# Source order for VectorE and ScalarE in the gated-input stage of a streaming encoder layer, with small changes at its start and its end

## The chip, the cores and the metric

One core of a Trainium2 chip runs the whole layer in one launch. The metric is the device time of an execution in microseconds (us). Before the change it is 1996.45 us, the median of 3 runs (1996.19 to 1996.85).

## What is computed

A conformer layer for 256 prompt frames and 8 x 16 sample frames, 384 rows in all, in float32:

```python
h   = rmsnorm(x)
proj = h @ w_in          # GLU in | q | k | v | forget logits | gate A | gate B
u = glu_in[..., :D_CONV] * sigmoid(glu_in[..., D_CONV:])
a_out = silu(layernorm(causal_dwconv(ext(u), 31 taps))) @ conv_pw_out
b_out = attn_fn(rmsnorm(q), rmsnorm(k), v, log_sigmoid(f_logit)) @ w_att_out
x = x + (sigmoid(gate_a) * a_out + sigmoid(gate_b) * b_out) @ w_out
x = x + (silu(causal_dwconv(g_half, 3 taps)) * u_half) @ w_down     # of rmsnorm(x) @ w_up
```

There are 8 heads of 128. A prompt frame looks at the prompt up to itself, a sample frame at 128 cached frames of its stream and at its own 16. D_MODEL is 2048, D_CONV 1024, D_FF 5632.

## The kernel before

Every product with weights is made of three TensorE passes: the float32 weights are split by ScalarE into a rounded part `hi` (L148, a cast) and by VectorE into the rest `lo` (L149), activations likewise, and hi x hi, hi x lo and lo x hi are added in PSUM (L245 to L247 where the activations are stationary, L250 to L252 in the other form). Weights come as tiles `raw` of two k blocks, fetched in the order of a plan (L139, SyncE's queue) and split two to three tiles ahead of their use by `ahead`; 3 tiles of `raw`, 3 of `hi` and 3 of `lo` are held.

`gemm` walks over jobs; after each k block it calls `tick`, which advances side work by one step. In the **gated-input stage** (L778 and after) four jobs of 16 k blocks make 64 ticks of 12 matmuls of 384 columns; each job fills four accumulators `acc` and ends, at ticks 15, 31, 47 and 63, with an evacuation by `glu_evac`: two VectorE products into `sgb`, two sigmoids of ScalarE, and two VectorE products into `ut`. Beside it run two generators. `conv` issues the 31 taps of the causal convolution on VectorE (L754), from tick 24 on. `attention` runs the 8 heads, one every 6 ticks: for head h at tick 6h+6 `head_operands` (VectorE transposes the cached keys `kc` into `kTs`, L611, and copies the queries into `qz`), at 6h+9 `head_scores` (TensorE scores L622 to L630 into three PSUM tiles, VectorE adds the bias `bs` and takes the maximum, ScalarE the exponentials `pr`), at 6h+14 `head_probs` (TensorE transposes L649 and L652; ScalarE copies one result into `pT`, L650, and VectorE the other into `pz`, L653), at 6h+17 `head_out` and at 6h+19 `head_last`. The PSUM tiles of these steps, `misc`, come from a ring of three, and so the second score tile (L624) needs `pT` of the head before copied out, and the third one (L626, L630) its `pz`. The cached keys and values and the bias rows of the heads are loaded by SyncE's queue (`load_k`, four DMAs into one of two `kc`; `load_v`; `load_b`); the loads of the next head's keys are issued with `head_operands`.

The order within an engine is that of a scheduler, which goes by priorities: a step written under `high_priority(offset=n)` counts as if it stood n instructions earlier. Weight splits and fetches have 150 (SPLIT_AHEAD), attention steps 250 (ATT_AHEAD), evacuations of accumulators 400 (EVAC_AHEAD). TensorE alone is held to the order of the source. `queued` ties an instruction behind the one of its engine that was given to it before, and so orders the instructions given to it.

At the **start** everything is written in order (L302 to L330): x comes in chunks of 128 columns, its 256 prompt rows by one DMA and its 128 sample rows by another, all on SyncE's queue, among the first weight rows. `x_chunk` transposes one chunk on TensorE and scales it into `hT` (ScalarE L297, VectorE L298). At the **end** the down projection is added into `y` in tiles of 128 x 512, and each tile of the last sum goes out by a DMA of SyncE's queue (L1052, L1055).

Of the kernel before, what the change touches and what calls it, by code (L numbers as in the profile page):

```python
# [19 lines left out]
H = 8  # L20
# [13 lines left out]
SPLIT_AHEAD, ATT_AHEAD, EVAC_AHEAD = 150, 250, 400  # L34
# [6 lines left out]
def hybrid_step(  # L41
# [36 lines left out]

    mm = nc.tensor.matmul
    tr = nc.tensor.transpose  # L80
    tt = nc.vector.tensor_tensor
    stt = nc.vector.scalar_tensor_tensor
    ts = nc.vector.tensor_scalar
# [15 lines left out]
    def load_x(c, n):  # L99
# [12 lines left out]
    def newton_rsqrt(r, s, m):  # L112
        queued(nc.scalar.activation(s, m, AF.Sqrt), in_first())
        nc.vector.reciprocal(r, s)
# [31 lines left out]
    def split_rows(hi, lo, raw, o, k):  # L146
        first = in_first()
        queued(nc.scalar.copy(hi[:, k, :o], raw[:, k, :o]), first)  # L148
        queued(tt(lo[:, k, :o], raw[:, k, :o], f(hi[:, k, :o]), op=ALU.subtract), first)  # L149
# [77 lines left out]
    def gemm(jobs, sides=(), wide=False):  # L227
        for js in jobs:
# [4 lines left out]
            for j, k in [(j, k + i) for k in range(0, js[0]["nk"], 2) for j in js for i in range(2)]:  # L233
# [29 lines left out]
    def blocks(rows, put):  # L263
        src = rows.rearrange("p t (m b j) -> p b m t j", m=4, b=4)
        for b in range(4):
            for a in range(4):
                nc.vector.transpose(put(a, slice(32 * b, 32 * b + 32)), src[32 * a:32 * a + 32, b])  # L267
# [22 lines left out]
    def x_chunk(c):  # L290
# [5 lines left out]
        with tc.high_priority(offset=EVAC_AHEAD):  # L296
            queued(nc.scalar.activation(hi, ps[:, :NT], AF.Identity, scale=g))  # L297
# [4 lines left out]
    with tc.manual_schedule(engines={ENG.SP, ENG.Activation, ENG.DVE}):  # L302
        nc.vector.memset(junk[:, 0:1], 0.0)
# [18 lines left out]
        nc.vector.tensor_copy(gm[:], pv[:, :16])  # L322
# [3 lines left out]
        warm_up(FILL)  # L326
        split_rows(hi, lo, first, V_COLS[0][0][1], slice(1, 2))
        x_chunk(1)
# [11 lines left out]
    def over_partitions(dg, dst):  # L340
# [3 lines left out]
        nc.scalar.copy(dst, ps[:, :NT])  # L344
# [46 lines left out]
    def small_columns():  # L391
        ps = misc_tile()
        tr(ps[:, :R_N], vrow[:R_N, :], ident[:R_N, :R_N])
        nc.vector.tensor_copy(col[:], ps[:, :R_N])
        ts(qgs[:], col[:, R_QG:R_QG + 1], float(P) ** -0.5, None, op0=ALU.mult)

    def first_norm():
        for c in range(2, 16, 2):
# [6 lines left out]
            if c % 4 == 2:  # L405
                for t in range(NTT):
                    n = c // 4
                    sq = nc.scalar.activation(junk[:], xs[n][:, t, :], AF.Square, accum_out=ssx[:, t, n:n + 1])
# [9 lines left out]
        with tc.high_priority(offset=EVAC_AHEAD):  # L418
            nc.vector.tensor_reduce(mt[:], ssx[:], axis=mybir.AxisListType.X, op=ALU.add)
            ts(mt[:], mt[:], 1.0 / DM, EPS, op0=ALU.mult, op1=ALU.add)  # L420
            r = rsqrt(mt[:], [P, NTT], p_x0, "r1")
            nc.vector.tensor_copy(rs1[:], r[:])
# [14 lines left out]
    def tok_job(dst, c0, n, sq):  # L437
        d = job("B", 16, ha, tok_evac(dst, c0, n))

        def post():  # L440
            for t in range(NTT):
                for h in range(c0 // P, (c0 + n) // P):
                    jk = p_qkv.tile([P, P], F32, tag="jk", bufs=2, name="jk")
                    nc.scalar.activation(jk[:], dst[:, t, h * P:(h + 1) * P], AF.Square,
# [4 lines left out]
    def tok_evac(dst, c0, n, shared=True):  # L449
        def ev(t, ps):  # L450
            if shared and t % 2:
                ts(dst[:, t, c0:c0 + n], ps[:, :n], rs1[:, t:t + 1], None, op0=ALU.mult)
            else:
                queued(nc.scalar.activation(dst[:, t, c0:c0 + n], ps[:, :n], AF.Identity, scale=rs1[:, t:t + 1]),
# [16 lines left out]
    nc.scalar.activation(e[:], e[:], AF.Exp, scale=-1.0)  # L471
    ts(r[:], e[:], 2.0, None, op0=ALU.add)
    nc.vector.reciprocal(r[:], r[:])
# [27 lines left out]
    def bias_rows():  # L501
        for _ in range(6):
            yield
        for i in range(2):
# [3 lines left out]
            nc.vector.tensor_copy(cw[:, i * 124:(i + 1) * 124], ps[:, :124])  # L508
            nc.vector.tensor_copy(fw[:, i * 66:(i + 1) * 66], ps[:, 128:128 + 66])
# [5 lines left out]
        nc.scalar.activation(crow[:, :2 * P], ps[:H, :2 * P], AF.Copy, scale=-1.0)  # L515
        ps = misc_tile()
        mm(ps[:H, :P], lg[:, 2, :], bm[:], start=True, stop=True)
        nc.scalar.activation(crow[:, 2 * P:], ps[:H, :P], AF.Copy, scale=-1.0)
# [3 lines left out]
        nc.scalar.copy(drow[:], ps[:64, :P])  # L522
# [18 lines left out]
    def q_panel(n):  # L541
        blocks(qt[:, :, 512 * n:512 * (n + 1)], by_feature(attT[:, 4 * n:4 * n + 4]))
        for h in range(4 * n, 4 * n + 4):
            nc.scalar.activation(attT[:, h], attT[:, h], AF.Identity, scale=qgs[:])
# [64 lines left out]
    def head_past_keys(d):  # L609
        kTs = p_att.tile([P, 8, P], F32, tag="kTs", bufs=1, name="kTs")  # L610
        nc.vector.transpose(kTs[:].rearrange("p b k -> p (b k)"), kcs[d["h"]][:])  # L611
        d["kTs"] = kTs

    def head_operands(d):
        head_past_keys(d)
        d["bs"] = bss[d["h"]]
        nc.vector.tensor_copy(qz[d["h"] % 2][:, :, :, 0:16], by_stream(attT[:, d["h"], 2 * P:]))
# [489 lines left out]
```

## Time and profile before

| what | us |
|---|---|
| median of 3 runs | 1996.45 |
| the profiled execution's own time | 1998.56 |
| its span from first to last instruction | 1996.7 |
| TensorE busy | 1986.5 |
| VectorE busy | 1305.3 |
| ScalarE busy | 743.2 |
| idle time of TensorE put down to a wait, longest single one | 2.5 |

The profile is one execution. Its times start at the first instruction, and its own time lies 1.9 us above its span and 2.1 us above the median of the runs. In its rows PE is TensorE's matmuls, PEld its weight loads, DVE is VectorE, ACT ScalarE, POOL GpSimd, SPq the issue of DMAs by SyncE. A row of the timeline has the start, the duration, engine, line and operation, what it writes and reads, how many in a row, and in brackets the idle time just ahead of it and what ended it. A row of the windows has the busy share of each engine in a stretch, then the granted TensorE clock as a share of the full one, the mean share of the 16 DMA engines, and their GB/s.

### The profile page before, as it was taken

Reading aid. Unit: us, or ns where it says so; the run is one execution under the profiler, and the core shown is the slowest. Engines: PE = TensorE matmul, PEld = TensorE weight load, DVE = VectorE, ACT = ScalarE, POOL = GpSimd, SP = SyncE. Lnnn points to the kernel's source line nnn. Section 1 sums busy time; section 2 is a strip of 40 time slices with the busy share of each in tenths; the row PEclk is TensorE's granted clock in tenths of the full one; section 3 lists DMA queues with packets and bytes.
Section 4 is the critical chain, followed back from the end, with each engine's and each line's share of the span. In section 5 each row is a group of like instructions: output and inputs, shape, how many; then the busy total and the mean of one; then the engine's idle time right before and its main releaser. Section 6 shows DMA issues by size and latency. Waiting matters only on the chain.

```text
span 1996.7 us, 24449 instructions
## 1 busy us (share of the span) xinstructions
PE 1986.5 (99%) x9383; PEld 1676.0 (84%) x9383; DVE 1305.3 (65%) x1908; ACT 743.2 (37%) x1077; POOL 89.5 (4%) x216
## 2 busy tenths in 40 slices
PE   9999999999999999999999999999999999999999
PEld 9888999888888888888888888888888888888887
DVE  4455889788755487676867683377673376638663
ACT  5535354433334433344333432233332233323321
POOL 1000011100000000000000000010000000000000
PEclk9999999999999999999999999999999999999999
DMA  6564767444443334534344443444433444343443
GB/s 184 149 188 117 216 154 161 141 140 131 130 129 124 128 125 163 165 122 137 119 137 126 129 134 129 129 126 127 136 129 132 132 118 137 128 133 120 138 158 106
DMA packets 209254, 275.98 MB, mean 138 GB/s; under 512 B 55878, under 2 KB 96729, under 8 KB 209129
## 3 DMA queue, kind: packets, MB, share of 16 engines
q1 hardware_dynamic: 208817, 273.85, 46.0%
q8 instruction: 73, 1.20, 0.3%
q0 software_dynamic: 288, 0.57, 0.1%
q14 instruction: 44, 0.36, 0.1%
q10 hardware_dynamic: 32, 0.01, 0.0%
HBM read 266.98 MB, written 7.86 MB: 138 GB/s over the span
## 4 chain that ended last, share of the span: by engine, by line
PE 96%; DVE 2%; DMA 1%; issue 0%; SPq 0%; ACT 0%; DVEq 0%; ACTq 0%
PE acc L252 20%; PE acc L250 20%; PE acc L251 20%; PE misc L252 10%; PE misc L251 10%; PE misc L250 10%; PE acc L245 2%; PE acc L247 2%; PE acc L246 2%; DVE lo L149 1%; DMA raw<-in_w_in_dram 0%; DVE mixT L267 0%; DVE ut L754 0%; DMA vc<-in_cache_v_dram 0%; DMA bs<-c_dr 0%
## 5 line engine op out<-in xcount | busy, mean ns | idle before, releaser
L149 DVE TENSOR_TENSOR lo<-raw,hi 128x1024 fp32r<-128x1024 f32 (+2 forms) x481 | 580.5, 1207 | 530.7 <-ACT hi L148 526.8
L148 ACT CAST hi<-raw 128x1024 fp32r<-128x1024 f32 (+2 forms) x481 | 496.3, 1032 | 970.1 <-PE misc L252 841.1
L250 PE MATMUL acc<-hi,xg 128*128 128x512 f32 x704 | 274.9, 390 | 0.0
L252 PE MATMUL acc<-hi,xg 128*128 128x512 f32 x704 | 273.9, 389 | 0.0
L251 PE MATMUL acc<-lo,xg 128*128 128x512 f32 x704 | 273.9, 389 | 0.0
L250 PE MATMUL acc<-hi,hT 128*128 128x512 f32 (+1 forms) x512 | 193.0, 377 | 0.5 <-ACT hT L297 0.5
L252 PE MATMUL acc<-hi,hT 128*128 128x512 f32 (+1 forms) x512 | 190.4, 372 | 0.2
L251 PE MATMUL acc<-lo,hT 128*128 128x512 f32 (+1 forms) x512 | 190.3, 372 | 0.0
L250 PEld LDWEIGHTS acc<-hi,xg 128*128 128x128 f32 x704 | 132.1, 188 | 28.4
L754 DVE SCALAR_TENSOR_TENSOR ut<-ext,cw,ut 128x384 f32<-128x384 f32 x240 | 151.9, 633 | 6.0
L252 PEld LDWEIGHTS acc<-hi,xg 128*128 128x128 f32 x704 | 132.1, 188 | 27.5
L251 PEld LDWEIGHTS acc<-lo,xg 128*128 128x128 f32 x704 | 132.2, 188 | 27.1
L252 PE MATMUL misc<-hi,xg 128*128 128x512 f32 x352 | 137.0, 389 | 0.0
L250 PE MATMUL misc<-hi,xg 128*128 128x512 f32 x352 | 137.0, 389 | 0.0
L251 PE MATMUL misc<-lo,xg 128*128 128x512 f32 x352 | 136.9, 389 | 0.0
L250 PE MATMUL acc<-hi,act 128*128 128x512 f32 x352 | 136.9, 389 | 0.0
L251 PE MATMUL acc<-lo,act 128*128 128x512 f32 x352 | 136.9, 389 | 0.0
L252 PE MATMUL acc<-hi,act 128*128 128x512 f32 x352 | 136.9, 389 | 0.0
L267 DVE STREAM_TRANSPOSE extf<-tok 32x384 f32<-32x384 f32 x176 | 100.3, 570 | 30.9 <-ACT tok L988 28.2
L267 DVE STREAM_TRANSPOSE uT<-tok 32x384 f32<-32x384 f32 x176 | 100.3, 570 | 29.7 <-ACT tok L988 26.9
L250 PEld LDWEIGHTS acc<-hi,hT 128*128 128x128 f32 x512 | 96.2, 188 | 16.1 <-ACT hT L297 1.0
L252 PEld LDWEIGHTS acc<-hi,hT 128*128 128x128 f32 x512 | 96.1, 188 | 15.7 <-DVE hT L298 0.7
(325 smaller groups left out, 3133.8 us busy)
## 6 DMA issues: line engine op xcount, KB each, us to landing
raw<-in_w_up_dram SPq DMA_DIRECT2D x176, 512.0 KB
raw<-in_w_in_dram SPq DMA_DIRECT2D x96, 512.0 KB
raw<-in_w_down_dram SPq DMA_DIRECT2D x88, 512.0 KB
raw<-in_w_in_dram SPq DMA_DIRECT2D x64, 256.0 KB
raw<-in_w_out_dram SPq DMA_DIRECT2D x32, 512.0 KB
raw<-in_w_att_out_dram SPq DMA_DIRECT2D x16, 512.0 KB
raw<-in_conv_pw_out_dram SPq DMA_DIRECT2D x16, 512.0 KB
raw<-in_w_in_dram SPq DMA_DIRECT2D x23, 344.0 KB
```

Source lines behind the costliest of these rows:

```text
L148: queued(nc.scalar.copy(hi[:, k, :o], raw[:, k, :o]), first)
L149: queued(tt(lo[:, k, :o], raw[:, k, :o], f(hi[:, k, :o]), op=ALU.subtract), first)
L245: mm(o, hi[:, kk, s], ah, start=st, stop=False)
L246: mm(o, hi[:, kk, s], al, start=False, stop=False)
L247: mm(o, lo[:, kk, s], ah, start=False, stop=sp)
L250: mm(o, ah[:, s], hi[:, kk, :n], start=st, stop=False)
L251: mm(o, ah[:, s], lo[:, kk, :n], start=False, stop=False)
L252: mm(o, al[:, s], hi[:, kk, :n], start=False, stop=sp)
L267: nc.vector.transpose(put(a, slice(32 * b, 32 * b + 32)), src[32 * a:32 * a + 32, b])
L754: stt(o, v, wc, o, op0=ALU.mult, op1=ALU.add)
```

## The change

1. All VectorE and ScalarE calls go through a wrapper, `InOrder`. While the list `chained` holds something, each instruction is tied behind the one before it on its engine. The list is filled just ahead of the gated-input jobs and emptied after the last attention step; the evacuations of accumulators in `gemm` are exempt and keep their priority.
2. The attention steps lose their priority of 250. The scaling of the probabilities becomes a step of its own, one tick after the scores, with one reciprocal of 3 columns for three of 1. `load_k` comes two heads ahead in place of one, `load_b` with the scaling step; these loads, `load_v` and `load_state` get the priority of weight fetches.
3. At the start ScalarE's queue loads the sample rows of the first two x chunks, ScalarE's first activation follows behind them, and the second `x_chunk` comes ahead of the split of the second weight row.
4. At the end the very last tile is added and stored in two halves of 256 columns, the second by ScalarE's queue.

```diff
+    chained = []
+    class InOrder:
+        def __getattr__(self, name):
+            op = getattr(self.eng, name)
+            def call(*a, **kw):
+                d = op(*a, **kw)
+                if chained:
+                    queued(d)
+                return d
+            return call
+    dve, act = InOrder(nc.vector), InOrder(nc.scalar)
...
+    def load_x(c, n, sample=nc.sync):
...
-        queued(nc.sync.dma_start(xs[c // 4][:, 2, o:o + n * P], xin[2][:, cs]))
+        queued(sample.dma_start(xs[c // 4][:, 2, o:o + n * P], xin[2][:, cs]))
...
                 if sp:
+                    held, chained[:] = chained[:], []
                     with tc.high_priority(offset=EVAC_AHEAD):
-                        for m in range(nb):
+                        for m in range(len(ps)):
                             j["evac"](m, ps[m])
+                    chained[:] = held
...
-        nc.scalar.activation(junk[:, 1:2], junk[:, 0:1], AF.Identity)
-        load_x(0, 1)
         first = stream_tile()
         fetch_row(first, plan[0], 0)
-        load_x(1, 1)
+        load_x(1, 1, nc.scalar)
+        act.activation(junk[:, 1:2], junk[:, 0:1], AF.Identity)
...
+        x_chunk(1)
         split_rows(hi, lo, first, V_COLS[0][0][1], slice(1, 2))
-        x_chunk(1)
...
-            nc.vector.reciprocal(mx[:, i:i + 1], mx[:, 6 + i:7 + i])
-            nc.scalar.activation(v, v, AF.Identity, scale=mx[:, i:i + 1])
+    def head_scale(d):
+        pr, mx = d["pr"], d["mx"]
+        dve.reciprocal(mx[:, 0:3], mx[:, 6:9])
+        for i, (_, o, n) in enumerate(d["segs"]):
+            v = pr[:, o * P:(o + n) * P]
+            act.activation(v, v, AF.Identity, scale=mx[:, i:i + 1])
...
-                with tc.high_priority(offset=ATT_AHEAD):
-                    step(d)
-                if step is head_operands and d["h"] + 1 < H:
-                    load_k(d["h"] + 1)
-                if step is head_probs and d["h"] + 2 < H:
-                    load_b(d["h"] + 2)
+                step(d)
+                with tc.high_priority(offset=SPLIT_AHEAD):
+                    if step is head_operands and d["h"] + 2 < H:
+                        load_k(d["h"] + 2)
+                    if step is head_scale and d["h"] + 2 < H:
+                        load_b(d["h"] + 2)
...
+    load_k(1)
...
+    chained.append(True)
     gemm([job("A", 16, ha, glu_evac(g)) for g in range(4)], [att_steps, conv_steps])
     drain(att_steps)
+    chained.clear()
...
-                tt(ys, ps[:], ys, op=ALU.add)
+                parts = [(0, 512)] if not last or n < 3 or t < 2 else [(0, 256), (256, 256)]
+                for o, w in parts:
+                    tt(ys[:, o:o + w], ps[:, o:o + w], ys[:, o:o + w], op=ALU.add)
```

TensorE's instructions stand in the same order in both kernels. Three places on the other engines, in the order in which each engine issues them, follow. In the changed kernel all wrapped calls have the wrapper's line, L89; the numbers in tile names count up in the order of the source.

The first place is VectorE ahead of the last head's scores. `kTs_3409` and `kTs_3395` are the last head's keys, `lo_3513` and `lo_3493` the split of the weights that the tick of these scores fetches, `misc_3457` and `misc_3443` the transposed probabilities of the head before. Before:

```order
L149 TENSOR_TENSOR lo_3435<-raw_3431,hi_3434 128x1024
L754 SCALAR_TENSOR_TENSOR ut_1998<-ext_3079,cw_753,ut_1998 128x384
L653 COPY pz0_1992<-misc_3457 128x8x16
L754 SCALAR_TENSOR_TENSOR ut_1998<-ext_3079,cw_753,ut_1998 128x384
L149 TENSOR_TENSOR lo_3513<-raw_3509,hi_3512 128x1024
L611 STREAM_TRANSPOSE kTs_3409<-kc_3211 128x1024
```

After:

```order
L89 STREAM_TRANSPOSE kTs_3395<-kc_3020 128x1024
L89 COPY qz1_1991<-attT_150 128x8x16
L89 SCALAR_TENSOR_TENSOR ut_1998<-ext_2556,cw_753,ut_1998 128x384
L89 SCALAR_TENSOR_TENSOR ut_1998<-ext_3074,cw_753,ut_1998 128x384
L89 COPY attT_150<-misc_3412 128x128
L89 SCALAR_TENSOR_TENSOR ut_1998<-ext_2556,cw_753,ut_1998 128x384
L89 SCALAR_TENSOR_TENSOR ut_1998<-ext_3074,cw_753,ut_1998 128x384
L89 TENSOR_TENSOR lo_3421<-raw_3417,hi_3420 128x1024
L89 COPY pz0_1992<-misc_3443 128x8x16
```

The key transpose has moved from behind the weight split of the scores' own tick to its own tick, three ticks ahead of the scores.

The second place is ScalarE at the first evacuation, tick 15, where head 0's `pT` and head 1's scores lie too. `hi_2300` and `hi_2310` are the split of the weights fetched at tick 14. Before:

```order
L148 CAST hi_2261<-raw_2258 128x1024
L148 CAST hi_2300<-raw_2297 128x1024
L650 COPY pT_2316<-misc_2317 128x512
L707 ACT_TABLE_LOAD
L707 ACTIVATE sgb_2345<-sgb_2345 128x384
L707 ACTIVATE sgb_2348<-sgb_2348 128x384
```

After:

```order
L89 CAST hi_2271<-raw_2268 128x1024
L89 ACT_TABLE_LOAD
L89 ACTIVATE sgb_2348<-sgb_2348 128x384
L89 ACTIVATE sgb_2351<-sgb_2351 128x384
L89 CAST hi_2310<-raw_2307 128x1024
L89 COPY pT_2326<-misc_2327 128x512
L89 ACT_TABLE_LOAD
```

The evacuation's sigmoids have moved ahead of the cast of tick 14 and of `pT`. VectorE has the same shift there: its products into `sgb_2348`, `sgb_2351` and `ut_1998` now follow on `kTs_2287`, the keys of head 1, and stand ahead of `lo_2311` (the rest of `hi_2310`) and `pz0_1992`.

The third place is SyncE's queue around the fetch of the weights of tick 14 (`raw_2297` before, `raw_2307` after) and the keys of heads 2 and 3. Before:

```order
L139 DMA raw_2258<-in_w_in_dram 128x2x256 x2
L724 DMA sc_2000<-in_state_conv_dram 30x8x32 x3
L139 DMA raw_2297<-in_w_in_dram 128x2x256 x2
L724 DMA sc_2000<-in_state_conv_dram 30x8x32
L139 DMA raw_2390<-in_w_in_dram 128x2x256 x2
L597 DMA bs_2326<-c_dr_755 128x128
L598 DMA bs_2326<-c_dr_755 128x256
L599 DMA bs_2326<-c_dr_755 128x128
L600 DMA bs_2326<-d_dr_756 128x1x128
L587 DMA kc_2460<-in_cache_k_dram 32x32x32
```

After:

```order
L156 DMA raw_2268<-in_w_in_dram 128x2x256 x2
L606 DMA kc_2149<-in_cache_k_dram 32x32x32 x4
L616 DMA bs_2249<-c_dr_755 128x128
L617 DMA bs_2249<-c_dr_755 128x256
L618 DMA bs_2249<-c_dr_755 128x128
L619 DMA bs_2249<-d_dr_756 128x1x128
L606 DMA kc_2290<-in_cache_k_dram 32x32x32 x4
L156 DMA raw_2307<-in_w_in_dram 128x2x256 x2
L156 DMA raw_2387<-in_w_in_dram 128x2x256 x2
```

The fetch of tick 14 has moved behind the four key loads of head 3, `kc_2290`, whose buffer comes free when `kTs_2287` has read it.

More of the change, by code (lines that the diff above doesn't have):

```diff
@@ L147, in split_rows @@
         first = in_first()
-        queued(nc.scalar.copy(hi[:, k, :o], raw[:, k, :o]), first)
+        queued(act.copy(hi[:, k, :o], raw[:, k, :o]), first)
         queued(tt(lo[:, k, :o], raw[:, k, :o], f(hi[:, k, :o]), op=ALU.subtract), first)
@@ L610, in head_past_keys @@
         kTs = p_att.tile([P, 8, P], F32, tag="kTs", bufs=1, name="kTs")
-        nc.vector.transpose(kTs[:].rearrange("p b k -> p (b k)"), kcs[d["h"]][:])
+        dve.transpose(kTs[:].rearrange("p b k -> p (b k)"), kcs[d["h"]][:])
         d["kTs"] = kTs
@@ L793, in hybrid_step @@
         hi, lo = aHL[h // 4][:, 0, h % 4, :], aHL[h // 4][:, 1, h % 4, :]
-        nc.scalar.copy(hi, attT[:, h, :])
+        act.copy(hi, attT[:, h, :])
         tt(lo, attT[:, h, :], f(hi), op=ALU.subtract)
```

135 lines of the change are left out of this document (69 added, 66 removed).

## The prediction

> **What bounds the kernel now.** I read the page first: the engines' busy time, then the chain that ended last.
>
> ```profile
> PE 1986.5 (99%) x9383; PEld 1676.0 (84%) x9383; DVE 1305.3 (65%) x1908; ACT 743.2 (37%) x1077; POOL 89.5 (4%) x216
> PE 96%; DVE 2%; DMA 1%; issue 0%; SPq 0%; ACT 0%; DVEq 0%; ACTq 0%
> ```
>
> TensorE is busy for 1986.5 of 1996.7 us, so the change can win only what TensorE waits, or runs slowly, around the places it touches. The waits of PE, longest first:
>
> ```profile
> PE misc L630 <- DVE kTs L611: 2.5, 1, 2.5
> PE misc L317 <- POOL ident L109: 1.5, 1, 1.5
> PE misc L884 <- DVE sgA L878: 0.5, 2, 0.3
> PE acc L250 <- ACT hT L297: 0.5, 1, 0.5
> ```
>
> One wait of 2.5 us lies in the gated-input stage, at the scores against cached keys; the other rows are the start and a later stage. The timeline at this wait:
>
> ```profile
> 349.72 1.04 ACT L148 CAST hi<-raw 128x1024 fp32r<-128x1024 f32 x1 [1.47 <-PE acc L246]
> 350.80 1.22 DVE L149 TENSOR_TENSOR lo<-raw,hi 128x1024 fp32r<-128x1024 f32 x1 [1.26 <-ACT hi L148]
> 351.94 1.24 DVE L611 STREAM_TRANSPOSE kTs<-kc 128x1024 f32<-128x1024 f32 x1
> 353.23 0.64 PE L630 MATMUL misc<-kTs,qz 128*32 128x128 f32 x15 [2.50 <-DVE kTs L611]
> ```
>
> VectorE stood idle for 1.26 us behind a `lo` whose `hi` was late, with the key transpose queued behind it: a matter of order, not of load. The clock after it, by windows of 1 us:
>
> ```profile
> 354.00:355.00 1.00, 1.00 (x5) 1.00 (x5) 0.71 (x7) 0.98 (x2) 0.00 (x0) 0.70 1.09 374
> 355.00:356.00 1.00, 1.00 (x4) 1.00 (x4) 0.11 (x1) 0.99 (x4) 0.00 (x0) 0.50 0.91 295
> 356.00:357.00 1.00, 1.00 (x4) 1.00 (x4) 0.05 (x1) 0.64 (x3) 0.00 (x0) 0.50 1.13 332
> 357.00:358.00 1.00, 1.00 (x5) 1.00 (x5) 0.00 (x0) 0.00 (x0) 0.00 (x0) 0.60 0.65 148
> 358.00:359.00 1.00, 1.00 (x8) 1.00 (x7) 0.00 (x0) 0.00 (x0) 0.00 (x0) 1.00 0.10 12
> ```
>
> The granted clock falls to half behind the wait: 0.3 + 0.5 + 0.5 + 0.4 = 1.7 us more are lost. The wait's whole price is 2.5 + 1.7 = 4.2 us.
>
> **What goes.** In the changed order the last head's `kTs` stands three ticks ahead of its scores and nothing of a later tick can stand ahead of it. A tick lasts over 2 us, `kTs` 1.24, so the wait and its slow clock go: **-4.2 us** (bounds: 0 if a wait just takes its place, -4.2).
>
> At the start, second x chunk first:
>
> ```profile
> 7.73 0.57 ACT L297 ACTIVATE hT<-misc,gm 128x384 fp32r<-128x384 f32 x1
> 8.36 0.42 PE L250 MATMUL acc<-hi,hT 128*128 128x344 f32 x1 [0.46 <-ACT hT L297]
> 15.18 0.43 PE L252 MATMUL acc<-hi,hT 128*128 128x344 f32 x1
> 8.00:9.00 1.00, 0.58 (x2) 0.31 (x2) 0.96 (x2) 0.86 (x2) 1.00 (x6) 1.00 1.22 230
> ```
>
> `hT` waited behind the cast of row 1. It now goes ahead, but the same matmuls then want that cast, which waits for its DMA, and the DMA engines are already taken in full (share 1.22). Two rows a queue earlier gain little there: **-0.4 us**, between 0 and the window's missing 0.42 plus its 0.46 of wait and a little at 15.18, -1.1. On this place the Trainium skill ("Trainium Kernel Development and Optimization", Key Constraints) says that DMAs issued from several queues run on the same 16 engines, and that several issuers only save issue time. By that rule the term would be nearer to 0; the share of 1.22 agrees.
>
> At the end:
>
> ```profile
> 1992.33 0.69 DVE L1052 TENSOR_TENSOR y<-misc,y 128x512 f32<-128x512 f32 x1
> 1991.69 1.69 SPq L1055 DMA_DIRECT2D out_dram<-y  x3
> 1993.00:1994.00 1.00, 0.00 (x0) 0.00 (x0) 0.03 (x1) 0.00 (x0) 0.00 (x0) 1.00 1.04 375
> ```
>
> The add of half a tile ends at most 0.35 us earlier, but behind it the engines carry the two tiles before at share 1.04, so the bytes set the end: **-0.1 us** (-0.5 to +0.2, the upper end for one more issue).
>
> The new `head_scale` saves two small reciprocals per head on a VectorE that no PE wait other than the one above names: 0.
>
> **What comes in its place.** First scores (tick 9):
>
> ```profile
> 234.75 0.57 DVE L267 STREAM_TRANSPOSE qt<-kt 32x384 f32<-32x384 f32 x1
> 236.40 0.65 PE L630 MATMUL misc<-kTs,qz 128*32 128x128 f32 x16
> ```
>
> Before, head 0's `kTs` was made long ahead, by priority. Now it stands behind the last transpose of the key panels (end 235.32). With 1.24 us of its own and 0.2 for `qz` it is ready at 236.8, wanted at 236.40: **+0.4 us** (0 to 1).
>
> Tick 15 is the costly place. Before:
>
> ```profile
> 237.47 0.99 SPq L139 DMA_DIRECT2D raw<-in_w_in_dram  x2
> 244.08 1.22 DVE L149 TENSOR_TENSOR lo<-raw,hi 128x1024 fp32r<-128x1024 f32 x1 [1.51 <-ACT hi L148]
> 248.23 0.29 DVE L653 COPY pz<-misc 128x128 f32<-128x128 f32 x1
> 248.77 1.10 DVE L706 TENSOR_TENSOR sgb<-acc,rs1b 128x384 f32<-128x384 f32 x2 [0.24 <-PE acc L247]
> 250.02 0.94 ACT L707 ACTIVATE sgb<-sgb 128x384 f32<-128x384 f32 x2
> 250.81 0.38 PE L626 MATMUL misc<-qt,attT 128*128 128x128 f32 x2
> ```
>
> `pz` was out at 248.5, and L626, which takes its PSUM tile, ran at 250.81 without a wait. Now the evacuation stands ahead. By order alone: the second `sgb` product ends at 249.87, its sigmoid (half of 0.94) at 250.34, the cast `hi` 1.04 later at 251.38, `lo` 1.16 later at 252.5, `pz` 0.29 later at 252.8. That is 2.0 us behind 250.81.
>
> The queue makes it worse. The weights that this `hi` reads, fetched at 237.47 before, now stand behind four key loads that wait until `kTs` of head 1 is done. This `kTs` follows on the `lo` of 244.08: 245.3 + 0.4 (tick 9's shift) + 1.24 = 246.9. What the loads take, from other heads' rows:
>
> ```profile
> 271.42 0.97 SPq L587 DMA_DIRECT2D kc<-in_cache_k_dram  x2
> 280.87 0.88 SPq L139 DMA_DIRECT2D raw<-in_w_in_dram  x2
> 283.43 1.05 ACT L148 CAST hi<-raw 128x1024 fp32r<-128x1024 f32 x1 [1.47 <-DMA raw<-in_w_in_dram]
> 337.46 3.21 SPq L587 DMA_DIRECT2D kc<-in_cache_k_dram  x4
> 340.00:341.00 1.00, 1.00 (x9) 1.00 (x10) 1.00 (x5) 1.00 (x3) 0.49 (x1) 1.00 1.34 207
> 341.00:342.00 1.00, 1.00 (x7) 1.00 (x7) 1.00 (x2) 1.00 (x2) 1.00 (x2) 1.00 1.28 147
> ```
>
> Four key loads take 1.9 us to issue (3.2 at worst), so the fetch is issued at 248.8. From issue to the cast are 2.56 us (280.87 to 283.43) on free engines: 251.4. But the keys' 512 KB move at only 147 to 207 GB/s with the engines full, 2.5 to 3.5 us, and about half of that lies beside the fetch: 252.8 (251.4 to 254). Then `hi` 253.8, `lo` 255.0, `pz` 255.3. L626 would want it at 251.2: **+4.1 us** (2.0 by order alone, to 5.4).
>
> In these 4 us TensorE does the one score that needs no `pz`, and stands idle over 3. The wait of 2.5 us cost 1.7 us of clock behind it, so this one costs that too: **+1.7 us** (0 to 3.4, two such stretches; I give the drop 8 in 10). Here a page speaks otherwise of the size: the Trainium skill, "TensorE: Matmul & The Clock Gate", summary of Part 1 and its rules, halves the clock after a free-running window of about 3.4 us without work, and asks for no gaps above about 3 us. The trace halves it behind 2.5 us of idle time, so here the trace decides. By the page a wait of 2.0 us would cost no clock, and order alone would give +2.0 and no more.
>
> Tick 27 repeats it more mildly. The keys of head 5, waiting for `kTs` of head 3, stand between the two halves of the weights of tick 26, and the cast of these (283.43 before) stands ahead of the copy of `pT`:
>
> ```profile
> 284.06 0.38 PE L626 MATMUL misc<-qt,attT 128*128 128x128 f32 x2
> ```
>
> If the weights land at 283.2 as before, `hi` ends at 284.3, `lo` at 285.4, `pz` at 285.7: 1.6 us late against 284.06. The waits ahead give the other engines some time to catch up, so I take **+1.2 us** (0 to 3). The evacuations at ticks 31, 47 and 63 have the scores of no head on the same tick, and cost 0. So do the taps on VectorE, which are on nobody's path until the stage has ended; if they are, a tap costs 0.6 us.
>
> **The sum.** -4.2 - 0.4 - 0.1 + 0.4 + 4.1 + 1.7 + 1.2 = +2.7 us. Against the profiled execution's own 1998.56 (span 1996.7) that makes 2001.3. That execution lies 2.1 us above the median of the runs, so against the median of 1996.45 it makes **1999.2 us**.
>
> **The rivals.**
> - *The wait just goes.* The fetch and the evacuation's order are hidden after all, for instance because ScalarE and VectorE run further ahead than I laid out. -4.2 - 0.4 - 0.1 = -4.7, 1991.8 us. For it speaks that before no score waited on `pz`; against it, that 2.0 us at tick 15 follow from the order and durations alone. 12 in 100.
> - *Order alone.* The fetch comes in time, only the evacuation delays `pz`, and 2.0 us of idle time do not halve the clock: -4.7 + 0.4 + 2.0 = -2.3, 1994.2 us. 14 in 100.
> - *A second slow stretch* (slower). At tick 27 the split fetch is late by the full 3 us. It decides from a wait of about 2.5 us on, since that one was followed by half clock: 3.0 + 1.7 in place of 1.2, +6.2 in all, 2002.7 us. For it: the half fetch is issued behind loads that run at 147 GB/s; against it: VectorE and ScalarE have slack by then. 22 in 100.
> - *The change does not reach the wait*: VectorE's new order excludes it, and I give it nothing of its own.
>
> **How the numbers follow.** My forecast has 52 in 100, with a range of its own from 1996.9 to 2001.3. A measurement can tell about 0.2% from no change, 4.0 us, so that "faster" is under 1992.5 and "slower" above 2000.4. Of the forecast, 8 in 100 lie above 2000.4, with the second slow stretch 30 are slower. Of the first rival 10 are faster and 2 within; order alone is within: 60 within, 10 faster. The range of 8 in 10 goes from 1992.0 (the wait goes, almost for nothing) to 2003.5 (the second stretch with a little more at tick 15).
>
> **What would show it.** The row L630 <- kTs of 2.5 us is gone from PE's waits, and the clock at the last head is 1.0. A new row appears, PE L624 or L626 waiting for `pT` or `pz`, of 3 to 4 us at about 251, with the cast ahead released by the DMA of `raw`, and windows at a clock of 0.5 behind it; a smaller one near 290. In SyncE's queue four key loads are issued at 247 and the weights behind them at 249. If that cast is released by PE or ScalarE itself, my queue term is wrong, and order alone holds. If PE shows no wait over 1 us between 236 and 260, the whole of what I add is wrong. A start that gains over 1 us or an end that gains over 0.5 would show that I have the DMA engines' share too tight.

## The result, and the profile after

The changed kernel takes 2007.89 us, the median of 6 runs (2007.28 to 2009.01), against 1996.68 us of the kernel before (6 runs, 1996.19 to 1998.59): 11.2 us slower, ratio 1.0055 with a 95% interval from 1.0042 to 1.0068. The forecast was 1999.2 with a range up to 2003.5; the time lies 8.7 us above the forecast and 4.4 us above its range. The size of the loss is less sure than the interval says: when the kernel before was run again beside the later experiments, its medians were 1998.20 (21 runs), 1997.69 and 1997.88 (27 runs each), with single runs from 1995.99 to 1999.52. The changed kernel ran beside the first 6 runs alone; against the later medians it is 9.7 to 10.2 us slower.

The page of the changed kernel, first the busy time of each engine, then the chain that ended last:

```profile
PE 1990.0 (99%) x9383; PEld 1678.0 (84%) x9383; DVE 1303.4 (65%) x1893; ACT 742.1 (37%) x1077; POOL 86.9 (4%) x216
PE 95%; DVE 3%; DMA 1%; issue 1%; ACT 0%; SPq 0%; DVEq 0%; ACTq 0%
```

The span is 2005.6 us, 8.9 more than in the profile before, and TensorE's busy time has grown by 3.5 us though it does the same matmuls: part of the loss is slow clock, the rest is waiting. What PE waited for, in total, times and longest:

```profile
PE misc L643 <- ACT pT L89: 7.1, 2, 5.0
PE misc L336 <- POOL ident L126: 1.5, 1, 1.5
PE misc L645 <- DVE pz L89: 0.9, 2, 0.6
PE misc L912 <- DVE sgA L89: 0.5, 2, 0.3
```

The 2.5 us for the last head's keys are gone, and so are the 0.5 us for `hT` at the start. In their place stand two waits for `pT` (L643 is the L624 of before: the second score tile). The timeline of SyncE, VectorE, ScalarE and TensorE around tick 15:

```profile
244.50 1.24 DVE L89 STREAM_TRANSPOSE kTs<-kc 128x1024 f32<-128x1024 f32 x1
245.76 2.41 SPq L606 DMA_DIRECT2D kc<-in_cache_k_dram  x4
248.27 8.06 SPq L156 DMA_DIRECT2D raw<-in_w_in_dram  x8
248.53 1.06 ACT L89 ACTIVATE sgb<-sgb 128x384 f32<-128x384 f32 x2 [3.91 <-DVE sgb L89]
249.33 0.38 PE L641 MATMUL misc<-qt,attT 128*128 128x128 f32 x2
253.12 1.04 ACT L89 CAST hi<-raw 128x1024 fp32r<-128x1024 f32 x1 [3.53 <-DMA raw<-in_w_in_dram]
254.07 0.58 ACT L89 COPY pT<-misc 128x512 f32<-128x512 f32 x1
254.71 1.22 PE L643 MATMUL misc<-qt,attT 128*128 128x256 f32 x2 [5.00 <-ACT pT L89]
```

This reads as one line of dominoes. `kTs` ends at 245.7, and only then SyncE issues the four key loads that wait for its buffer; the weights of tick 14, fetched at 237.47 before, are issued behind them at 248.27, and the cast that reads them starts 4.85 us later; ScalarE has been through with the sigmoids since 249.6 and stands 3.53 us in front of the cast, with `pT` queued behind it; TensorE stands 5.00 us in front of its second score. The clock behind it, by windows:

```profile
253.00:254.00 1.00, 0.00 (x0) 0.00 (x0) 0.00 (x0) 0.88 (x1) 0.00 (x0) 0.81 1.03 363
254.00:255.00 1.00, 0.29 (x1) 0.29 (x2) 0.80 (x1) 0.98 (x3) 0.00 (x0) 0.50 0.86 303
259.00:260.00 1.00, 1.00 (x5) 1.00 (x4) 0.04 (x1) 0.93 (x1) 0.00 (x0) 0.50 0.14 37
260.00:261.00 1.00, 1.00 (x6) 1.00 (x5) 1.00 (x1) 0.00 (x0) 0.00 (x0) 0.77 0.25 60
```

The granted clock falls to half while PE still waits, and it stays there until after 260, so the scores themselves run at half speed too. Tick 27 repeats the pattern with the second half of the fetch of tick 26:

```profile
285.10 2.21 SPq L606 DMA_DIRECT2D kc<-in_cache_k_dram  x4
287.36 0.79 SPq L156 DMA_DIRECT2D raw<-in_w_in_dram  x1
291.41 1.04 ACT L89 CAST hi<-raw 128x1024 fp32r<-128x1024 f32 x1 [8.75 <-DMA sc<-in_state_conv_dram]
292.99 0.70 PE L643 MATMUL misc<-qt,attT 128*128 128x256 f32 x2 [2.07 <-ACT pT L89]
```

The row of the cast names the load `sc`, which was issued behind that half fetch; the cast itself reads `raw`, so that it waited for the weights is inferred here (in e3 the same row names `raw`).

And the last head's scores, where the long wait of before was, still wait once:

```profile
363.16 0.49 PE L645 MATMUL misc<-qt,attT 128*128 128x128 f32 x2 [0.63 <-DVE pz L89]
```

TensorE does the same instructions in the same order in both kernels, so the start of one matmul in both traces gives the balance up to there. The first matmul of some ticks:

| matmul | before, us | after, us | difference | what lies between it and the row above |
|---|---|---|---|---|
| tick 10 | 236.98 | 236.15 | -0.83 | start -1.13; `kTs` and `qz` of head 0, +0.30 |
| tick 16 | 251.70 | 257.48 | +5.78 | first wait and its slow scores, +6.61 |
| tick 18 | 257.55 | 264.69 | +7.14 | half clock, +1.36 |
| tick 27 | 281.20 | 288.34 | +7.14 | nothing |
| tick 28 | 284.94 | 295.26 | +10.32 | second wait, +3.18 |
| tick 30 | 290.79 | 302.35 | +11.56 | half clock, +1.24 |
| tick 51 | 347.49 | 359.50 | +12.01 | ticks 39 and 45, +0.45 |
| tick 52 | 353.80 | 364.15 | +10.35 | wait for `kTs` gone (-2.50), 0.63 for `pz` new, 0.21 not traced: -1.66 |
| tick 54 | 361.23 | 370.00 | +8.77 | half clock of before gone, -1.58 |
| end of the span | 1996.7 | 2005.6 | +8.9 | the end, +0.13 |

The profiles differ by 8.9 us, the medians by 11.2. The first experiment shows where the difference comes from.

### The profile page after: what moved, and what is told of

Its sections match the earlier page's. It is cut to its first block, busy times and chain, and to the rows that moved or that the text cites. A ratio compares the mean times of both kernels' runs of the same rounds, so it can differ in the third digit from the quotient of the medians.

```text
span 2005.6 us, 24439 instructions
## 1 busy us (share of the span) xinstructions
PE 1990.0 (99%) x9383; PEld 1678.0 (84%) x9383; DVE 1303.4 (65%) x1893; ACT 742.1 (37%) x1077; POOL 86.9 (4%) x216
## 4 chain that ended last, share of the span: by engine, by line
PE 95%; DVE 3%; DMA 1%; issue 1%; ACT 0%; SPq 0%; DVEq 0%; ACTq 0%
PE acc L267 20%; PE acc L269 20%; PE acc L268 20%; PE misc L269 10%; PE misc L267 10%; PE misc L268 10%; PE acc L262 2%; PE acc L263 1%; PE acc L264 1%; DVE lo L89 1%; DVE qt L89 0%; DVE mixT L89 0%; DVE sgA L89 0%; DVE ut L89 0%; PE misc L312 0%
## 5 line engine op out<-in xcount | busy, mean ns | idle before, releaser
L89 DVE TENSOR_TENSOR lo<-raw,hi 128x1024 fp32r<-128x1024 f32 (+2 forms) x481 | 580.1, 1206 | 537.9 <-ACT hi L89 534.1
L89 ACT CAST hi<-raw 128x1024 fp32r<-128x1024 f32 (+2 forms) x481 | 495.9, 1031 | 952.1 <-PE misc L269 824.4
L89 DVE SCALAR_TENSOR_TENSOR ut<-ext,cw,ut 128x384 f32<-128x384 f32 x240 | 148.7, 638 | 3.7
L89 DVE STREAM_TRANSPOSE extf<-tok 32x384 f32<-32x384 f32 x176 | 100.3, 570 | 30.9 <-ACT tok L89 28.2
L89 DVE STREAM_TRANSPOSE uT<-tok 32x384 f32<-32x384 f32 x176 | 100.3, 570 | 29.7 <-ACT tok L89 26.9
```

The costliest lines, as they stand in the source:

```text
L89: d = op(*a, **kw)
```

## The experiments

Two theories stood against each other. **Q**: weight fetches stand in SyncE's queue behind loads that wait for a buffer, because these loads now have the fetches' priority; all the rest follows. **O**: the order on ScalarE and VectorE (source order, evacuations ahead) makes the waits. Beside them, what the start, the end and the earlier keys do by themselves.

### e1: the kernel before, once more

No edit.

> The kernel before, run again for its spans and clocks. The two profiles differ by 8.9 us of span (1996.7 and 2005.6), the medians by 11.2. Theory A: the half clock behind the 2.5 us wait comes only in some executions of the kernel before, and its profile showed such a one: most executions then have a span near 1994.6 to 1995.0 with a mean clock above 0.999 and a time near 1996.5, and this profile shows the wait of 2.5 us with the clock at 1.0 behind it. Theory B: the half clock is in every execution and the 2.1 us lie elsewhere: every span lies near 1996.7 or the profile shows 0.5 in the windows behind the wait though the time is near 1996.5.

10 executions of it took 1995.91 to 1999.11 us (ratio 0.9998, 0.9989 to 1.0007); the profiled one took 1995.91, with a span of 1994.1. Its waits, and the windows behind the wait at the last head:

```profile
PE misc L630 <- DVE kTs L611: 2.5, 1, 2.5
```

```profile
353.00:354.00 1.00, 1.00 (x8) 1.00 (x7) 0.72 (x6) 1.00 (x1) 0.66 (x2) 1.00 1.07 353
354.00:355.00 1.00, 1.00 (x8) 1.00 (x7) 0.68 (x5) 0.99 (x5) 0.00 (x0) 1.00 1.09 358
355.00:356.00 1.00, 1.00 (x7) 1.00 (x6) 0.00 (x0) 0.45 (x3) 0.00 (x0) 1.00 1.12 337
```

The same wait of 2.5 us, and no slow clock behind it: the half clock is not in every execution, as theory A says. But A also expected most executions near 1996.5, and 8 of the 10 lie above 1997.1; that part failed. This trace also reaches tick 10 at 235.78, 1.20 us before the first one, at the start alone. So one kernel has executions that differ by 1.2 us at its start and by 1.6 at its last head. The profile from which the prediction was made had both losses. Its 1998.56 us are 2.1 above the median of the first 3 runs, but only 0.4 to 0.9 above the later medians: those 3 runs were low ones. Against this second trace, the fastest of its 10, the changed kernel's span is 11.5 us longer.

### e2: keys one head ahead again

```diff
-                with tc.high_priority(offset=SPLIT_AHEAD):
-                    if step is head_operands and d["h"] + 2 < H:
-                        load_k(d["h"] + 2)
+                if step is head_operands and d["h"] + 1 < H:
+                    load_k(d["h"] + 1)
+                with tc.high_priority(offset=SPLIT_AHEAD):
...
-    load_k(1)
```

> The changed kernel with the key loads put back to one head ahead and without the fetch priority. Theory Q (the weights of ticks 14 and 26 are fetched behind the key loads in SyncE's queue, and that alone makes the two waits): both waits for pT vanish (5.0 and 2.1 us) with their pz waits and the two half-clock stretches, 12.4 us less by the sums of the two profiles, so about 1995.5 us. Theory O (the evacuation ahead of pT and the strict source order make the waits): tick 27, which has no evacuation, still shows its wait of 2 to 3 us, and the time lies near 2000 to 2004.

1996.40 us (11 runs), ratio to the kernel before, run beside it (1998.20), 0.9992, interval 0.9983 to 1.0001. The waits of this run that lie in the stage:

```profile
PE misc L645 <- DVE pz L89: 1.0, 2, 0.6
PE misc L764 <- ACT pT L89: 0.7, 1, 0.7
PE misc L649 <- DVE qz L89: 0.3, 1, 0.3
```

Both long waits are gone, also the one of tick 27, which has no evacuation near. That is Q. The time is 0.9 us above what Q expected. In this run the scheduler moved `pT` and `pz` back ahead of the evacuation too, so for tick 15 it does not tell the two apart.

### e3: evacuations in source order

```diff
-                    held, chained[:] = chained[:], []
                     with tc.high_priority(offset=EVAC_AHEAD):
...
-                    chained[:] = held
```

> The changed kernel with the evacuations held to the source order too, so that pT and pz stand ahead of the first evacuation, and the key loads left as they are. Theory Q: the cast ahead of pT still waits for its weights until about 253, so the wait of 5.0 us at tick 15 and the one of 2.1 us at tick 27 stay, about 2008 us (or a little more, since the accumulators come free later). Theory O: the wait at tick 15 is gone with its slow clock, 8.0 us less, about 2000 us.

2010.24 us (5 runs), ratio 1.0061 (1.0049 to 1.0074). Its waits, and ScalarE at tick 15, where `pT` now stands ahead of the sigmoids:

```profile
PE misc L641 <- ACT pT L89: 8.8, 2, 5.0
```

```profile
252.59 1.04 ACT L89 CAST hi<-raw 128x1024 fp32r<-128x1024 f32 x1 [9.80 <-DMA raw<-in_w_in_dram]
253.55 0.58 ACT L89 COPY pT<-misc 128x512 f32<-128x512 f32 x1
255.60 0.52 ACT L89 ACTIVATE sgb<-sgb 128x384 f32<-128x384 f32 x1 [0.17 <-DVE sgb L89]
```

The evacuation's place, O's part of tick 15, is put right and the wait is 5.0 us as in the changed kernel: the cast in front of `pT` still waits for its weights. From tick 10 to tick 16 e3 takes 21.27 us and the changed kernel 21.33, so the evacuation's place costs nothing on top of the late weights. The wait at tick 27 is even longer, 3.8 us against 2.1; both halves of that fetch are issued behind the keys here (286.75 and 287.70), where the changed kernel has one.

### e4: no source order

```diff
-    chained.append(True)
```

> The changed kernel without source order in the gated-input stage, all else as changed (keys two heads ahead, no attention priority, start and end). The scheduler then puts the weights of tick 14 ahead of the keys in SyncE's queue, the last head's key transpose far ahead of its scores, and pT and pz ahead of the first evacuation. Theory Q: no wait over 1 us is left in the stage, and with the 1.1 us of the start the time falls below the kernel before, to 1992 to 1994 us. Rival: without its priority of 250 the attention falls behind and new waits for scores or probabilities of 2 to 5 us come, 1998 to 2003 us.

2011.71 us (5 runs), ratio 1.0068 (1.0056 to 1.0081): neither expectation. Four new waits, all of TensorE for the split `lo`, and ScalarE, VectorE and TensorE at the first of them:

```profile
PE acc L264 <- DVE lo L89: 12.1, 4, 4.2
```

```profile
270.68 1.97 ACT L89 CAST hi<-raw 128x1024 fp32r<-128x1024 f32 x2
273.21 1.51 DVE L89 SCALAR_TENSOR_TENSOR ut<-ext,cw,ut 128x384 f32<-128x384 f32 x2
274.64 1.21 DVE L89 TENSOR_TENSOR lo<-raw,hi 128x1024 fp32r<-128x1024 f32 x1
275.91 0.69 PE L264 MATMUL acc<-hT,lo 128*128 128x384 f32 x1 [2.73 <-DVE lo L89]
```

Tick 15 is free here, since its weights are fetched ahead of the keys (235.52 against 240.50). The new waits are not Q: two casts `hi` run from 270.68 to 272.65, so the weights are there, and VectorE works without a gap from 269.48 on. In its order taps of the convolution and copies of the attention stand ahead of the `lo` for which TensorE stands from 273.2 on. The other three waits look alike: the casts end 2.0 to 4.3 us before the wait does, and VectorE has taps (297.86, 339.55) or copies of the attention (318.33) ahead of `lo`. So the order on VectorE can stop TensorE by itself when the scheduler chooses it. The rival had the sizes about right (1.4 to 4.2 us) but not the place, and the time is above its 2003. Why the scheduler chose this order, the runs do not show.

### e5: the loads without the fetch priority

```diff
-                with tc.high_priority(offset=SPLIT_AHEAD):
-                    if step is head_operands and d["h"] + 2 < H:
-                        load_k(d["h"] + 2)
...
+                if step is head_operands and d["h"] + 2 < H:
+                    load_k(d["h"] + 2)
...
```

`load_b` and `load_v` are moved out in the same way; source order and keys two heads ahead stay.

> The changed kernel with source order and keys two heads ahead, but with the loads of keys, bias rows and values at their place in the source, without the fetch priority. The scheduler then puts the weights of tick 14 ahead of the keys of head 3 again. Theory Q (weight fetches stand behind loads that wait for a buffer): the waits of 5.0 and 2.1 us at ticks 15 and 27 go, the small ones of the source order at the last head (0.6) stay, about 1995 to 1998 us, no slower than the kernel before. Rival (source order itself makes the waits, wherever the loads stand): at least 4 us above the kernel before.

**1994.08 us** (11 runs, 1993.83 to 1994.22), ratio to the kernel before 0.9982 (0.9973 to 0.9991): faster than both kernels (the kernel before, run beside it, took 1997.69), and 0.9 us below the range that Q expected. SyncE around tick 14 and the waits that are left in the stage:

```profile
236.19 1.46 SPq L156 DMA_DIRECT2D raw<-in_w_in_dram  x2
237.70 2.71 SPq L606 DMA_DIRECT2D kc<-in_cache_k_dram  x3
```

```profile
PE misc L649 <- DVE qz L89: 0.3, 1, 0.3
PE misc L645 <- DVE pz L89: 0.2, 1, 0.2
```

The fetch is back at 236 and nothing over 0.3 us waits in the stage. Source order is not what made the changed kernel slow. Keys, bias rows and values were moved together here; e2, which moved the keys alone, already lost both long waits.

### e6 and e7: the kernel before with the keys two heads ahead, alone and with start and end

```diff
-                if step is head_operands and d["h"] + 1 < H:
-                    load_k(d["h"] + 1)
+                if step is head_operands and d["h"] + 2 < H:
+                    load_k(d["h"] + 2)
...
+    load_k(1)
```

> The kernel before with one edit: the keys are loaded two heads ahead, without any priority. In its order the last head's key transpose stands ahead of the split that held it up. Theory K (the 2.5 us wait needs only the early keys, not the source order): the wait is gone with what slow clock it brought, 2.5 to 4.1 us less than the kernel before, ratio 0.9980 to 0.9988. Rival: the earlier key loads displace weight fetches in SyncE's queue and a new wait of 2 us or more comes at another head, ratio 0.9995 or above.

> The run before this one with the start and the end of the change added. If the start gains by itself, tick 10 is reached at about 235.3 in the trace (as in the runs that have it, 235.3 to 235.9 once their 0.3 us at tick 9 is taken off), and the time is 0.5 to 1.1 us under the run before; if the start's gain was only the variation between executions (236.98 and 235.78 in two traces of the kernel before), the times of the two agree within 0.3 us. The end: from the last matmul's start to the end of the span 4.7 to 4.9 us in both.

2002.74 us (ratio 1.0023, 1.0014 to 1.0031) and 2001.09 us (1.0018, 1.0009 to 1.0026), 11 runs each. The wait at the last head is gone in both, and another has come at head 5. From e6:

```profile
314.17 2.28 SPq L139 DMA_DIRECT2D raw<-in_w_in_dram  x2
316.50 5.74 SPq L587 DMA_DIRECT2D kc<-in_cache_k_dram  x4
322.43 1.04 ACT L148 CAST hi<-raw 128x1024 fp32r<-128x1024 f32 x1 [4.77 <-DMA kc<-in_cache_k_dram]
326.59 0.49 PE L659 MATMUL misc<-vt,pT 128*128 128x128 f32 x2 [4.02 <-DVE mx L636]
```

Theory K holds for the wait that it was about and fails for the time: a new wait is there, in the size of the rival. Its reason is another one. The fetch does land late, 8.3 us from its start in SyncE's queue to the cast, 6.0 from the end of its issue. But TensorE waits for the maximum of head 5's scores, and this is VectorE's order. In the kernel before, the first of these maxima (L636) stood right behind three taps:

```profile
317.68 0.28 DVE L636 CUSTOM_DVE_ANT_0 pr<-misc,bs 128x128 f32<-128x128 f32 x1
```

In e6 thirteen taps, the next key transpose and a weight split stand ahead of it, and VectorE has no idle time put down to any wait from 314.71 to 326.25. From e6:

```profile
319.13 3.22 DVE L754 SCALAR_TENSOR_TENSOR ut<-ext,cw,ut 128x384 f32<-128x384 f32 x5
322.27 1.24 DVE L611 STREAM_TRANSPOSE kTs<-kc 128x1024 f32<-128x1024 f32 x1
323.93 1.22 DVE L149 TENSOR_TENSOR lo<-raw,hi 128x1024 fp32r<-128x1024 f32 x1
326.25 0.28 DVE L636 CUSTOM_DVE_ANT_0 pr<-misc,bs 128x128 f32<-128x128 f32 x1
```

So with the earlier keys the scheduler chose another order for VectorE, and that order made the wait. e7 has the same order and the same wait of 4.0 us. e5, which has source order and the other parts of the change, is 7.0 us faster than e7. The start and the end make 1.65 us between e6 and e7, more than the 0.5 to 1.1 expected; from the last matmul's start to the end of the span it is 5.0 and 5.2 us where 4.7 to 4.9 were expected, so none of it comes from the end.

### e8 and e12: how much of the late landing is the keys' small packets

In both runs keys and weights are tied in SyncE's queue in the order of the source, and the orders of all engines agree. e8 reads the keys in runs of 512 bytes, e12 in runs of 128.

```diff
-            nc.sync.dma_start(kc[q, :].rearrange("k (b j d) -> k b j d", b=8, j=4),
-                              cache_k[0, :, :, h, q].rearrange("b (j k) d -> k b j d", j=4))
+            queued(nc.sync.dma_start(kc[q, :].rearrange("k (b d) -> k b d", b=8),
+                                     cache_k[0, :, q, h, :].rearrange("b k d -> k b d")), bool(chained))
```

> The changed kernel with each key load as the same four DMAs of 128 KB, but read in runs of 512 bytes in place of 128, and with keys and weights tied in SyncE's queue in the order of the source, so that the weights of tick 14 stand behind the keys of head 3 as in the changed kernel. The cached keys then lie in another layout, so the scores against them are not those of the reference. Read at tick 15 alone. Theory C (the landing of the weights, 4.85 us after their issue in place of 2.56, is the keys' small packets in the same engines): the weights land 2.6 to 3.2 us after their issue, and the wait for pT shrinks from 5.0 to about 3.0 to 3.4 us. Rival (the place in the queue alone): landing and wait stay at 4.8 and 5.0.

> The twin of the run with long key runs: the same order on every engine and the same tie in SyncE's queue, but the keys read in runs of 128 bytes as in the changed kernel. Read at tick 15, where the fetch of the weights stands behind the four key loads in both. There the long runs gave 1.81 us of issue for the four loads and 3.87 us from the fetch's issue to the cast. Theory C (the keys' small packets take the engines from the fetch): 2.2 to 2.6 us of issue and 4.6 to 5.0 us from issue to cast, so that the wait for pT is 1.2 to 2 us longer than the 9.45 us with long runs. Rival (the place in the queue alone): issue, landing and wait within 0.3 us of the long runs' numbers.

Both expectations of e8 missed: the tie alone puts more bias loads and half of another fetch in front, and the wait for `pT` at tick 15 grew to 9.45 and 10.33 us, so e8 cannot be held against the changed kernel's 5.0; hence its twin. The fetch and the cast, first with long runs, then with short ones:

```profile
258.47 2.95 SPq L156 DMA_DIRECT2D raw<-in_w_in_dram  x6
262.34 1.04 ACT L89 CAST hi<-raw 128x1024 fp32r<-128x1024 f32 x1 [7.33 <-DMA raw<-in_w_in_dram]
```

```profile
259.93 3.08 SPq L156 DMA_DIRECT2D raw<-in_w_in_dram  x6
264.10 1.04 ACT L89 CAST hi<-raw 128x1024 fp32r<-128x1024 f32 x1 [8.16 <-DMA raw<-in_w_in_dram]
```

From issue to cast 3.87 and 4.17 us, the four key loads ahead of it took 1.81 and 2.33 us to issue. Short runs cost 0.3 + 0.5 = 0.8 us (0.88 by the two waits), less than the 1.2 to 2 expected of them; each number is from a single execution. Most of the delay, 3.87 against 2.56 on free engines, comes with long runs too. These two executions took 2022.37 and 2031.96 us, the longest times of all these kernels.

### e9: the evacuation ahead, the fetch early

From e5, with `hi` and `lo` of tick 14 held behind the first evacuation:

```diff
+    def follow(d, e):
+        tc.add_manual_dep(d.ins, e.ins.name, mybir.DependencyInfo(
+            mybir.DependencyClass.NoSync, mybir.DependencyReason.DATA), reason="queue")
...
+                if g == 0 and m == 1:
+                    follow(last_split[0], sig)
...
+                if g == 0 and m == 3:
+                    follow(last_split[1], pu)
```

> The run with source order and loads at their place (1994.1 us), with one order forced: at tick 15 ScalarE's cast and VectorE's split of the weights of tick 14 stand behind the first evacuation, as in the changed kernel, while SyncE fetches those weights early. This is the prediction's 'order alone'. By it pz comes 2.0 us late at tick 15 (about 1.5 to 2.5 us of PE waiting for pT and pz), and the time is 2.0 us up, to about 1996.1 us, with no slow clock behind it if a stretch needs about 2.5 us of waiting, and 1.4 to 1.7 us more if it needs less. Rival (the order costs nothing, only the late fetch did): no wait over 0.5 us at tick 15 and 1994.1 us.

1997.59 us (11 runs), 3.5 more than e5. PE at tick 15:

```profile
250.63 0.70 PE L650 MATMUL misc<-qt,attT 128*128 128x256 f32 x2 [1.35 <-ACT pT L89]
251.70 0.46 PE L652 MATMUL misc<-qt,attT 128*128 128x128 f32 x2 [0.37 <-DVE pz L89]
```

Tick 16 starts 2.2 us later than in e5's place (252.66 against 250.37, less 0.05 at tick 10): the order alone, with the fetch early, costs about what was laid out for it, 2.0. The 11 times fall in two groups, 5 from 1996.10 to 1996.44 and 6 from 1997.59 to 1997.95; the profiled one, 1996.21, has a clock of 1.0 throughout. The second group's 1.5 us fit a half-clock stretch, and its mean clock is 0.999 in all six (1.0 in four of the other five), but none of its executions was profiled.

### e10 and e11: e5 without the start, e5 without the halves

The edits undo parts 3 and 4 of the change.

> The same base (1994.1 us) without the change of the start: its times should go up by 0.4 to 1.6 us and scatter more (in three traces without the changed start tick 10 was reached at 235.8, 236.4 and 237.0, in five with it at 235.3 to 235.9 once the wait of tick 9 is taken off). If the start's gain was chance, the median stays within 0.3 us of the base.

> The same base (1994.1 us) with the last tile added and stored in one piece by SyncE's queue. The bytes set the end: within 0.3 us of the base, and 4.8 to 5.2 us from the last matmul's start to the end of the span. If the halves gain, 0.3 to 0.6 us slower than the base.

Without the start 1995.39 us (11 runs, 1994.85 to 1995.75): the start gains 1.3 us (1.4 against e11, which ran beside it), and the times spread over 0.4 us with it (e5) and 0.9 without. The two edits at the start, the queue and the order, were not separated. Without the halves 1994.01 us (1993.71 to 1994.22): 0.07 us better than with them, nothing that the runs can tell.

## Why the prediction was wrong

The mechanism at ticks 15 and 27 was forecast with its place and its engines, and it is shown (e2, e3, e5). Two terms of the sum failed: tick 27, and the two queue times at tick 15. A third part of the miss lies in the number that the sum was added to.

- **"If the weights land at 283.2 as before ... I take +1.2 us."** Measured +3.2, and 1.2 of half clock behind it for which the sum had nothing: 3.2 us too little, the largest miss. The step that failed is "as before". The keys stood in front of half of that fetch; it was issued 2.3 us behind the first of them, and the cast started 4.05 us later, with other loads beside it. The third score (L626 of before) started 2.8 us late where 1.6 were laid out. So of the miss 1.12 is the landing, 0.44 the credit taken for other engines catching up, 0.42 the scores at half speed and 1.24 the clock behind them. This is the rival named the second slow stretch (2002.7 us), which I gave 22 in 100 with the words that the engines have slack by then. They were idle, ScalarE 8.75 us and VectorE 5.70, but the next instruction of each stood behind the late weights, so the slack was of no use.
- **"L626 would want it at 251.2: +4.1 us."** Measured +6.6. TensorE came 1.2 us earlier than laid out, because the start had gained 1.1, for which the layout had nothing, and tick 9 lost 0.3 in place of 0.4. The keys' transpose came 1.2 us earlier too (245.74 against 246.9). The queue behind it did not keep up: from there to the issue of the fetch it took 2.5 us where 1.9 were laid out, and from issue to cast 4.85 where 4.0 were. So the weights landed 0.3 us after the 252.8 of the prediction, and the wait grew. Another 1.0 us went because the clock was at half while the scores still ran: 1.2 + 0.3 + 1.0 make the 2.5. The wait that ended last was that of the second score for `pT`, not that of L626 for `pz`.
- **"+1.7 us" of half clock at tick 15** was 1.4, beside the slow scores.
- **"The wait's whole price is 2.5 + 1.7 = 4.2 us."** 3.2 between the profiles: 0.63 for `pz` came in place, as a tap pair and a weight split now stand ahead of it. The prediction had put the taps on nobody's path. And the 1.7 us are in some executions only (e1).
- **"That execution lies 2.1 us above the median of the runs."** The prediction took these 2.1 us off as a constant. They were the slow clock and the slow start of one execution, and a median of 3 low runs; by the later medians 0.4 to 0.9 us would have been right. The changed kernel's profiled execution (2007.77) lies 0.1 below its median.
- **Start -0.4 us**: -1.1 between the profiles, but nothing against the second trace of the kernel before (e1: tick 10 at 235.78; the changed kernel without its 0.30 at 235.85). By medians it is -1.3 to -1.4 (e10). By the prediction's own sign, a gain above 1 us, the DMA engines' share was read too tight there. **End -0.1**: +0.1 in the profiles and 0.07 by e11. **Tick 9 +0.4**: 0.3. **Ticks 39 and 45**: 0.45 us, not foreseen.
- **"Order alone"**, 2.0 us: 2.2 in e9. But in the changed kernel it adds nothing, because the fetch lands later than the evacuation ends (e3).

Between the two profiles these terms make 6.2 of the 8.7 us by which the forecast missed, and the 2.1 us taken off make most of the rest.

The Trainium skill ("TensorE: Matmul & The Clock Gate", Part 1) calls the window of the clock gate free-running. The runs fit that part better than the gap of about 3 us in its rules: the same wait of 2.5 us was followed by half clock in one trace of the kernel before and not in the other. I had read one trace as the rule of the chip.

What stays open: how the 3.87 us of landing with long key runs divide between the bytes in front, the order in which the engines serve them and the later fetches, which in the changed kernel are issued right behind the late one (eight DMAs in the row at 248.27); no run takes that apart.

## What to carry to other kernels

A load that may have to wait for its buffer should not stand ahead of the stream that the bottleneck lives on, in an in-order queue: give it a place behind, however early its data are wanted. The same change without that priority was 3.6 us faster than the kernel before (e5), with it 11.2 slower, each against the kernel before that ran beside it. Look also at what the scheduler puts ahead of the bottleneck's operands on a busy engine: in e4, e6 and e7, without source order, taps and copies on VectorE stopped TensorE for up to 4.2 us. A price read from one profiled execution holds for the median only if that execution is like the median, and three runs are few to know the median by.

## What the runs showed of the hardware

- A wait of 2.5 us of PE was followed by half clock for over 3 us in one execution and by none in another of the same kernel (clock 0.50 and 1.00 in the windows behind it); in e9, whose profiled execution has waits of 1.35 and 0.37 us close together, the times fall in two groups 1.5 us apart.
- Weights of 512 KB that are cast 2.56 us after their issue on free engines were cast 3.87 to 4.85 us after it behind 512 KB of keys, and in e6 8.3 us after the start and 6.0 after the end of their issue, with the keys issued right behind them.
- The start of one and the same kernel reached tick 10 at 235.8 and 237.0 in two traces; with the sample rows on ScalarE's queue and the second chunk ahead, ten traces lie between 235.3 and 235.9, once the wait at tick 9 is taken off.
